# Rounded fp32 products that read and write from the last column to the first

## The chip, the cores and the metric

The kernel runs on one core of a Trainium2 chip. The metric is the device time of one execution in microseconds; lower is better. Beside the time there is a profile of one execution: every instruction of the engines TensorE (PE; its weight loads are listed apart as PEld), VectorE (DVE), ScalarE (ACT), GpSimd (POOL) and SyncE (SP), with the transfers. TensorE reads a stationary and a moving operand from the on-chip memory and adds its results into PSUM, a memory of eight banks of 512 fp32 columns on 128 partitions.

## The reference

One layer of a decoder block over 512 tokens of width 1024, in float32:

```
h = x + 1/2 * SwiGLU_1(RMSNorm(x))                 # D_FF = 2816
z = RMSNorm(h) @ W_in                              # q, three pairs of k/v, gates, S5 input u
o = concat(sparse_attention(z), S5(u)) @ W_out     # 8 heads of 64 in 2 groups; compressed,
h = h + o                                          #   selected and window branches, gated
h = h + 1/2 * SwiGLU_2(RMSNorm(h))
h = h + sigmoid(RMSNorm(h) @ W_gate) * (p @ W_ple)
out = RMSNorm(h)

def swiglu(x, w1, w3, w2):
    return (jax.nn.silu(x @ w1) * (x @ w3)) @ w2
```

Nearly all the arithmetic is in dense products of 128-row weight tiles with activations of 512 tokens.

## The kernel before

Activations lie transposed: features on the 128 partitions, the 512 tokens along the columns. So a product takes a 128x128 weight tile as stationary operand and 512 (or 256) token columns as moving operand, and writes as many columns of a PSUM bank.

To keep the accuracy of fp32, each fp32 operand `x` is split into two rounded fp32 (`float32r`, FR) parts, `hi = round(x)` and `lo = round(x - hi)`; `mm3` then makes three products into one PSUM group: hi with hi, hi with lo, lo with hi. Weights come in units of 128x1024 fp32 (`load_unit`, on ScalarE's DMA queue), are rounded by ScalarE (`hi`, line 164) and subtracted by VectorE (`lo`, line 166). `xh` and `xl` are the two halves of a normed activation, `hq` those of a SwiGLU's hidden tile, `oh` and `ol` those of the mixer's output, `sh` and `sl` those of the sums of blocks of the activation.

The stages in order of time are: the first SwiGLU (about 0 to 365 us, beside it the constants of the S5 mixer on POOL and VectorE), the projections by `W_in` with the S5 scan (365 to 480), the compressed keys and the scores (480 to 555), attention's values (`values`, 555 to 605) with the product by `W_out`, the second SwiGLU (656 to 980), the gate and the last norm. Both SwiGLUs make some of their "up" tiles by a scheme of seven block products in place of eight (`up_fast`): its products have 256 columns, and their results lie in halves of the banks A, B and D. The "down" products have 512 columns and write bank C. The banks are four tags, A to D, with two buffers each (`bank`); a bank is used again when its reader (ScalarE or VectorE) is done.

In `values`, a block of keys takes two products into a bank of tag C (`KA` with `QA`, `KB` with `QB`; a bf16 mask product is added on the diagonal), ScalarE takes the exponential, and two products with `VL` (`eh`, `el`) add to a bank of tag D.

Every product that is not a transpose is issued by the helper `mm`, so they all stand at line 133 in the profile and are told apart by the names of their tiles. The order of work on each engine is set when the program is built, by a scheduler with a cost model of its own, and `pinned` keeps chosen instructions in program order. The same step sets which semaphores an instruction waits for.

Some products are not of the kind that the change names: the bf16 warm-up products (`wz`) and masks, the plain fp32 products of the GLU (`yt` with `raw`) and of the compression (`raw` with `cs` and `turn`), the S5 products, products with 280 columns (values and gates), and transposes (lines 727, 1016, 1162, 1343). Line 1016 transposes the S5 output into PSUM columns that stand eight words apart:

```
p = bank(TP, (128, 64, 8))
for t in range(8):
    PE.transpose(p[:, :, t], yc[:, t], ident[:64, :64])
```

Of the kernel before, what the change touches and what calls it, by code (L numbers as in the profile page):

```python
# [11 lines left out]
FR = mybir.dt.float32r  # L12
# [64 lines left out]
def block_kernel(ctx: ExitStack, tc: tile.TileContext, a: dict, out: bass.AP):  # L77
# [14 lines left out]
    def bank(tag, shape=(128, 512), dt=F32):  # L92
        return psum.tile(list(shape), dt, tag=tag, name="ps_" + tag)
# [36 lines left out]
    pinned = tc.keep_in_program_order  # L130

    def mm(o, lhsT, rhs, start, stop, **kw):
        return PE.matmul(o, lhsT, rhs, start=start, stop=stop, **kw)  # L133


# [5 lines left out]
    for i in range(COLD):  # L141
        pinned(mm(cold, wz[:, :128], wz, True, True))

    def unit(raw_only=False, keep=None, q=nc.scalar, after=None, at=None):
        i = unit_i[0] if at is None else at
        if at is None:
            unit_i[0] += 1
        w = UNIT_W[i]
        if i not in raws:
            load_unit(i, q)  # L150
        raw = raws.pop(i)
        if raw_only:
            return raw
        return split(raw, (slice(0, w),), keep, after)
# [18 lines left out]
    def mm3(o, wh, wl, xh, xl, first, last, kept=free):  # L173
        kept(mm(o, wh, xh, first, False))
        kept(mm(o, wh, xl, False, False))
        kept(mm(o, wl, xh, False, last))
# [1273 lines left out]
    for m in range(KT):  # L1450
        if m % 4 == 0:
            wu = unit()
        o = bank("B")
# [18 lines left out]
    with tc.tile_pool(name="gate", bufs=2, reuse_waits="tile") as gp:  # L1472
# [15 lines left out]
        def products(i, wu, cs, kept=free, beside={}):  # L1488

            o = bank("AB"[i % 2])[:, :cs.stop - cs.start]  # L1490
            for k in range(KT):
                sl = slice(k * 128, (k + 1) * 128)
                for j, (w_, x_) in enumerate(((0, ng.xh), (0, ng.xl), (1, ng.xh))):
                    kept(mm(o, wu[w_][:, sl], x_[:, k, cs], k + j == 0, k == KT - 1 and j == 2))
                if k in beside:
                    beside[k]()
            return o
# [34 lines left out]
        for m in range(KT - 3):  # L1532
            o = products(m, unit(), slice(0, SEQ))
# [246 lines left out]
```

## Time and profile before

| what | value |
|---|---|
| median of three runs | 1042.88 us (1041.19 to 1043.49) |
| span of the profiled execution, first to last instruction | 1040.7 us; its own time outside the profiler is not listed |
| granted TensorE clock, mean | 0.997 |
| TensorE products | 1028.1 us busy, 6048 records |
| TensorE weight loads | 874.7 us, 6049 records |
| VectorE, ScalarE, POOL | 822.9, 506.2 and 161.3 us |
| products of 512 columns into bank C from `hq` | 1056 records, mean 389 to 390 ns each as modelled |
| products of 256 columns | mean 280 to 289 ns each as modelled |

The modelled length of a product is longer than its distance to the next, since products overlap in the array. A group that the timeline merges (x8) has the length from the first start to the last end. A record of a plain fp32 product is one of two in which the chip makes it.

### The profile page before, as it was taken

How to read it: one execution, taken by the hardware profiler on the slowest of the kernel's cores; microseconds unless marked ns; L12 is line 12 of the kernel's file. 1: busy time of each engine (PE TensorE's matmuls, PEld its weight loads, DVE VectorE, ACT ScalarE, POOL GpSimd, SP SyncE). 2: the span in 40 equal slices, each digit the busy share in tenths (PEclk: the TensorE clock that was granted, in tenths of full speed). 3: DMA queues.
4: the chain of work that ended last, by engine and by line, in shares of the span. 5: the costliest groups of instructions: out<-in, count | busy, mean ns of one | idle time of the engine just before them, and what ended most of it. 6: DMA issues, size and time to landing. Idle time of an engine off the chain costs nothing.

```text
span 1040.7 us, 15688 instructions
## 1 busy us (share of the span) xinstructions
PE 1028.1 (99%) x6048; PEld 874.7 (84%) x6049; DVE 822.9 (79%) x1382; ACT 506.2 (49%) x872; POOL 161.3 (15%) x181
## 2 busy tenths in 40 slices
PE   9999999999999999999999999999999999999997
PEld 6888888889889888776586688998999899899886
DVE  6798468988889766986698877996598588687676
ACT  6322232535336542667678855663365245255452
POOL 0003948207870200100000000000000000000001
PEclk9999999999999999999999999999999999999998
DMA  8424325646354639566510023333333333333412
GB/s 267 143 85 134 100 86 168 232 122 129 120 133 151 228 117 226 181 198 181 162 41 21 21 70 127 127 103 121 93 94 118 101 102 102 101 103 104 145 56 82
DMA packets 50618, 129.98 MB, mean 125 GB/s; under 512 B 10608, under 2 KB 17424, under 8 KB 50544
## 3 DMA queue, kind: packets, MB, share of 16 engines
q10 hardware_dynamic: 26352, 90.77, 28.2%
q0 software_dynamic: 6592, 18.48, 7.0%
q1 hardware_dynamic: 17600, 19.73, 6.1%
q8 instruction: 47, 0.77, 0.3%
q14 instruction: 27, 0.22, 0.1%
HBM read 112.81 MB, written 15.73 MB: 124 GB/s over the span
## 4 chain that ended last, share of the span: by engine, by line
PE 89%; DVE 3%; POOL 3%; DMA 2%; issue 2%; ACT 1%; SPq 0%; DVEq 0%; ACTq 0%; POOLq 0%
PE ps_A L133 27%; PE ps_C L133 25%; PE ps_B L133 20%; PE ps_D L133 16%; POOL ft L721 1%; POOL bt L720 1%; DMA raw<-in_wpack 1%; DMA cst<-kcd 0%; DVE lo L166 0%; DMA kcd<-ra 0%; POOL ft L719 0%; DVE s L342 0%; POOL seen L559 0%; DMA h<-in_xT 0%; PE ps_D L727 0%
## 5 line engine op out<-in xcount | busy, mean ns | idle before, releaser
L164 ACT CAST hi<-raw 128x1024 fp32r<-128x1024 f32 (+2 forms) x143 | 144.4, 1010 | 250.3 <-PE ps_C L133 92.6
L133 PE MATMUL ps_C<-hq,hi 128*128 128x512 f32 x704 | 217.6, 390 | 0.2
L166 DVE TENSOR_TENSOR lo<-raw,hi 128x1024 fp32r<-128x1024 f32 (+2 forms) x143 | 174.1, 1218 | 44.5 <-ACT hi L164 43.6
L133 PEld LDWEIGHTS ps_C<-hq,hi 128*128 128x128 f32 x704 | 130.8, 188 | 28.1 <-DVE h L526 1.3
L133 PE MATMUL ps_C<-hq,lo 128*128 128x512 f32 x352 | 136.9, 389 | 0.0
L133 PE MATMUL ps_A<-xh,hi 128*128 128x512 f32 (+1 forms) x352 | 124.5, 354 | 0.5 <-ACT hi L164 0.5
L133 PE MATMUL ps_A<-xl,hi 128*128 128x512 f32 (+1 forms) x352 | 124.1, 352 | 0.4 <-DVE xl L192 0.3
L133 PE MATMUL ps_A<-xh,lo 128*128 128x512 f32 (+1 forms) x352 | 122.5, 351 | 0.2 <-DVE lo L166 0.2
L164 ACT CAST hi<-s 128x1024 fp32r<-128x1024 f32 x56 | 59.0, 1053 | 107.1 <-PE ps_D L133 63.6
L166 DVE TENSOR_TENSOR lo<-s,hi 128x1024 fp32r<-128x1024 f32 x56 | 70.6, 1261 | 20.4 <-ACT hi L164 20.3
L133 PEld LDWEIGHTS ps_C<-hq,lo 128*128 128x128 f32 x352 | 66.1, 188 | 13.8
L133 PEld LDWEIGHTS ps_A<-xh,hi 128*128 128x128 f32 x352 | 66.5, 189 | 10.4 <-ACT hi L164 0.7
L133 PEld LDWEIGHTS ps_A<-xl,hi 128*128 128x128 f32 x352 | 66.5, 189 | 10.1 <-DVE xl L192 1.2
L133 PEld LDWEIGHTS ps_A<-xh,lo 128*128 128x128 f32 x352 | 66.5, 189 | 9.2 <-DVE lo L166 0.4
L526 DVE SCALAR_TENSOR_TENSOR h<-ps_C,h 128x512 f32<-128x512 f32 x64 | 43.9, 686 | 36.8 <-PE ps_C L133 36.6
L133 PE MATMUL ps_B<-sh,lo 128*128 128x256 f32 x224 | 63.1, 282 | 0.3 <-DVE lo L166 0.3
L133 PE MATMUL ps_D<-sl,hi 128*128 128x256 f32 x224 | 63.1, 282 | 0.0
L133 PE MATMUL ps_B<-sh,hi 128*128 128x256 f32 x224 | 63.0, 281 | 0.0
L133 PE MATMUL ps_B<-sl,hi 128*128 128x256 f32 x224 | 62.9, 281 | 0.0
L133 PE MATMUL ps_D<-sh,hi 128*128 128x256 f32 x224 | 62.8, 280 | 0.0
L133 PE MATMUL ps_B<-xh,hi 128*128 128x512 f32 (+1 forms) x168 | 62.8, 374 | 0.0
L133 PE MATMUL ps_D<-sh,lo 128*128 128x256 f32 x224 | 62.7, 280 | 0.0
(435 smaller groups left out, 2470.9 us busy)
## 6 DMA issues: line engine op xcount, KB each, us to landing
raw<-in_wpack ACTq DMA_DIRECT2D x168, 512.0 KB, 3.6
si<-s5i POOLq DMA_DIRECT2D x8, 512.0 KB, 5.2
so<-s5o POOLq DMA_DIRECT2D x8, 512.0 KB, 5.5
h<-in_xT SPq DMA_DIRECT2D x8, 256.0 KB, 4.1
s5i<-fs POOLq DMA_DIRECT2D x1, 2048.0 KB, 11.3
xraw<-in_xT SPq DMA_DIRECT2D x8, 256.0 KB, 3.4
s5o<-gt POOLq DMA_DIRECT2D x1, 2048.0 KB, 13.4
s5i<-tcs POOLq DMA_DIRECT2D x2, 1024.0 KB, 10.4
```

The source lines that it names most:

```text
L133: return PE.matmul(o, lhsT, rhs, start=start, stop=stop, **kw)
L164: p, q = S.copy(hi[:, c], raw[:, c]), None
L166: q = V.tensor_tensor(lo[:, c], raw[:, c], hi[:, c].bitcast(F32), OP.subtract)
L526: V.scalar_tensor_tensor(h[:, m, :], o[m], 0.5, h[:, m, :], OP.mult, OP.add)
L720: G.tensor_tensor(bt, b2[:, 1], bc(psn[:, e]), OP.mult)
L721: G.tensor_tensor(ft[:, :, s_, :], ft[:, :, s_, :], bt, OP.add)
```

## The change

`mm` reverses the column order of both sides of a product where the moving operand is rounded fp32, has two dimensions and 256 or 512 columns. Column n of the moving operand still lands in column n of the result; only the order in which the columns go through the array is turned. The stationary operand is left as it is.

```
     def mm(o, lhsT, rhs, start, stop, **kw):
+        if len(rhs.shape) == 2 and rhs.shape[1] in (256, 512) and rhs.dtype == FR:
+            o, rhs = o[:, ::-1], rhs[:, ::-1]
         return PE.matmul(o, lhsT, rhs, start=start, stop=stop, **kw)
```

Two lines more make line 133 into line 135 in the changed kernel. In the built program the access patterns of 2664 products of 512 columns and of 2496 of 256 columns begin at the last column and have a step of -1. The order of instructions is the same on every engine, and so are the waits of all engines but TensorE. There, waits on TensorE's own semaphore (PE_49) come and go. In the two pieces that follow, each row is a product with its result and operands, and in brackets the semaphores that it waits for.

On TensorE in `values`, at a head group's end and the next one's start, before:

```order
L133 MATMUL ps_D<-eh,VL 128x512 [waits Activation_49]
L133 MATMUL ps_C<-QA,KA 128x512
L133 MATMUL ps_C<-QB,KB 128x512
L133 MATMUL ps_D<-el,VL 128x512 [waits DVE_49]
L133 MATMUL ps_D<-eh,VLc 128x512 [waits PE_49,Activation_49]
```

The same rows of the changed kernel:

```order
L135 MATMUL ps_D<-eh,VL 128x512 [waits Activation_49]
L135 MATMUL ps_C<-QA,KA 128x512 [waits PE_49]
L135 MATMUL ps_C<-QB,KB 128x512
L135 MATMUL ps_D<-el,VL 128x512 [waits DVE_49]
L135 MATMUL ps_D<-eh,VLc 128x512 [waits Activation_49]
```

The first product into a bank of tag C now waits for TensorE's own earlier product there, and the first into the bank of tag D no longer does.

On TensorE in `up_fast`, where a half of bank D begins a new tile, before:

```order
L133 MATMUL ps_A<-xh,hi 128x256
L133 MATMUL ps_A<-xl,hi 128x256
L133 MATMUL ps_A<-xh,lo 128x256
L133 MATMUL ps_D<-sh_1758,hi 128x256
L133 MATMUL ps_D<-sl_1759,hi 128x256
```

The same rows of the changed kernel:

```order
L135 MATMUL ps_A<-xh,hi 128x256
L135 MATMUL ps_A<-xl,hi 128x256
L135 MATMUL ps_A<-xh,lo 128x256
L135 MATMUL ps_D<-sh_1758,hi 128x256 [waits PE_49]
L135 MATMUL ps_D<-sl_1759,hi 128x256
```

Here too the tile's first product waits for the product that last wrote the bank. In all, 63 products get such a wait and 18 lose one.

## The prediction

> **What bounds the kernel now.** I read the page first: its busy shares, its row of granted clock and the chain that ended last.
>
> ```profile
> PE 1028.1 (99%) x6048; PEld 874.7 (84%) x6049; DVE 822.9 (79%) x1382; ACT 506.2 (49%) x872; POOL 161.3 (15%) x181
> ...
> PEclk9999999999999999999999999999999999999998
> ...
> PE 89%; DVE 3%; POOL 3%; DMA 2%; issue 2%; ACT 1%; SPq 0%; DVEq 0%; ACTq 0%; POOLq 0%
> ```
>
> The reader is to see that TensorE is busy for 1028.1 of 1040.7 us at the full granted clock and makes 89% of the chain, so 12.6 us are all its idle time. Whatever a product takes more or less goes into the end time almost one to one: the next engine, VectorE, has 822.9 us of work, 218 us less than the span.
>
> What one product costs is the distance from its start to the next start, not its modelled length (0.28 or 0.39 us). The chain in order of time gives it, since it merges runs of products into one bank:
>
> ```profile
> 226.70 5.44 PE ps_B L133 x24
> 232.14 1.43 PE ps_A L133 x12
> ```
>
> The first row is 24 products of 512 columns: 5.44 / 24 = 0.227 us each. The second is 12 of 256 columns: 0.119 us each. Two reference rates stand beside them, the bf16 warm-up products near the end and the plain fp32 products of the GLU and of the compression:
>
> ```profile
> 1028.86 1.89 PE L133 MATMUL ps_C<-wz 128*128 128x512 bf16 x8
> ...
> L133 PE MATMUL ps_C<-wz x14: 376/378/379, 1028.9 to 1032.0; 128*128 128x512 bf16 x14
> ...
> L133 PE MATMUL ps_A<-yt,raw 128*128 128x512 f32 x32 | 14.8, 601 | 0.0
> ...
> 495.99 3.65 PE L133 MATMUL ps_A<-yt,raw 128*128 128x512 f32 x8
> ...
> 480.55 0.38 PE L133 MATMUL ps_A<-raw,cs 128*64 128x256 f32 x1
> ...
> 480.76 0.38 PE L133 MATMUL ps_A<-raw,cs 128*64 128x256 f32 x1
> ```
>
> Columns of the timeline rows are start, length of the merged group, engine and operation. Eight bf16 products with one 0.378 us tail: (1.89 - 0.38) / 7 = 0.216 us. So 512 columns stream in 0.216 us, and a rounded fp32 product has 0.011 us beyond that; at 256 columns it is the same (0.119 - 0.108). A record of plain fp32 moves at half that rate: (3.65 - 0.60) / 7 = 0.436 us for 512 columns, 480.76 - 480.55 = 0.21 us for 256.
>
> **The change, part by part.** No instruction is added, removed or moved in any engine's work, and no operand has other bytes. Three things differ.
>
> *The steps.* In the built program 2664 products of 512 columns and 2496 of 256 have a step of -1 instead of +1 in moving operand and result; the stationary operand, which PEld loads, keeps +1. In the profile they take 2664 x 0.227 + 2496 x 0.119 = 605 + 297 = 902 us, 87% of the span. Not reversed are all plain fp32 and bf16 products, the products of 280, 384 and 64 columns, and the scores of the early blocks, whose moving operand has three dimensions. If a step of -1 streams like +1, this part costs 5160 x 0 = 0.
>
> No row of before has a moving operand with a step other than +1 inside its runs. The nearest row for the result is the S5 transpose of line 1016, which writes 64 columns to words that stand 32 bytes apart, beside the transpose of line 727, which writes 128 consecutive ones:
>
> ```profile
> 476.63 0.71 PE L1016 MATMUL ps_D<-ident,ysb 64*128 64x64 f32 x8
> ...
> L1016 PE MATMUL ps_D<-ident,ysb x32: 221/223/273, 428.8 to 477.1; 64*128 64x64 f32 x32
> ...
> 131.09 1.09 PE L727 MATMUL ps_D<-ident,ft 128*128 128x128 f32 x8 [0.33 <-POOL ft L721]
> ```
>
> Scattered: (0.71 - 0.22) / 7 = 0.070 us for 64 columns, 1.09 ns a column with the fixed part in it. Consecutive: (1.09 - 0.27) / 7 = 0.117 us for 128, 0.91 ns a column. Taking 0.011 us off each leaves 0.92 and 0.83 ns: a result written word by word costs about a tenth more here, but at a pace half as fast as the rounded products run (0.216 / 512 = 0.42 ns). So these rows bound the price without deciding it. Lower end: 0. Upper end: every column as a word by itself at the whole 1.09 ns, 0.560 us for 512 and 0.280 for 256, which adds 2664 x 0.333 + 2496 x 0.161 = 1289 us and gives 2332 us. I take 0, the end that the contiguous rows give: columns 511, 510, 509 fall into the same short stretches of memory as 509, 510, 511, each stretch visited once and left for good, and only an address circuit that handles +1 alone would make more accesses of it. That is a judgement on the circuit, not a reading, and both ends stay in the chances.
>
> The Trainium skill speaks against this: "PSUM — Partial Sum Buffer", section "Specifications (TRN2)", gives PSUM lines of 8 bytes and says that any access pattern that isn't contiguous slows matmuls significantly. By it, if a step of -1 counts as not contiguous, two results no longer share an access, and the time would be that of the first rival below; the S5 row agrees only weakly, with its tenth.
>
> *The waits of TensorE on itself.* The order shows that TensorE's waits on its own semaphore change: 63 products get one, 18 lose one (39 before, 84 after), and 9 more of these stand as separate semaphore instructions. No wait of another engine changes. Each new wait is for the product that last wrote the PSUM bank about to be reused. Counted in products on TensorE, 36 of them look 36 to 108 products back (FFN, projections, W_out and the gate), 27 look 4 to 18 back (attention). A satisfied wait of this kind exists in before, on the product at 233.41:
>
> ```profile
> 233.29 0.28 PE L133 MATMUL ps_A<-xh,lo 128*128 128x256 f32 x1
> 233.41 0.28 PE L133 MATMUL ps_D<-sh,hi 128*128 128x256 f32 x1
> 233.53 0.28 PE L133 MATMUL ps_D<-sl,hi 128*128 128x256 f32 x1
> ...
> L1016 PEldq EVENT_SEMAPHORE  x1: 51/51/51, 439.6 to 439.6; - x1
> ...
> 439.39 0.40 PE L133 MATMUL ps_A<-xh,lo 128*128 128x512 f32 x1
> 439.62 0.40 PE L133 MATMUL ps_A<-xh,hi 128*128 128x512 f32 x1
> 439.86 0.39 PE L133 MATMUL ps_A<-xl,hi 128*128 128x512 f32 x1
> ...
> 443.82 0.70 PE L1016 MATMUL ps_D<-ident,ysb 64*128 64x64 f32 x8
> ```
>
> It starts 0.12 us after its neighbour, as the next does: cost 0. The 51 ns semaphore instruction for the transposes at 443.82 was done at 439.6, 18 products ahead, and the products around it start 0.23 to 0.24 us apart: hidden too. What is queued behind a waiting product is all of TensorE's later work, so the question is whether the product waited for has ended. With 36 or more products between, and a queue about 18 ahead, it has. With 4 between (the closest of the 27) it ended 0.39 us after its start, while the waiter's turn comes 4 x 0.23 = 0.92 us after it; 0.53 us are left, and a weight load takes 0.19 of them:
>
> ```profile
> 655.95 0.19 PEld L133 LDWEIGHTS ps_B<-xh,hi 128*128 128x128 f32 x1
> ```
>
> Moreover the bank's reader (ScalarE's exponential or VectorE) had to wait for the same product, and TensorE waits for that reader anyway. Cost taken: 0. Upper end, if this cover were gone and each of the 63 stalled until the product before it had drained, with a semaphore instruction each: 63 x (0.39 - 0.227 + 0.051) = 13.5 us. Lower end: the 18 waits that go were satisfied, so nothing comes back.
>
> *Order of the results in time.* A bank's readers wait for the last product of the group as a whole, whose end is the same whichever column comes last. No reader starts earlier or later: 0.
>
> The sum: 0 + 0 + 0. The profiled execution's span is 1040.7 us; the median of the three runs, 1042.88, stands 2.2 us above it, within which lie what is around the span and the spread of the runs (1041.19 to 1043.49). I forecast 1042.9 us, with an own range of 1040 to 1046. About 0.2% (2.1 us) is what a measurement of this kernel can tell from no change.
>
> **The rivals.**
>
> 1. *Half rate: the kernel becomes far slower.* Place: every reversed product. Mechanism: two columns per access go one way only, in the read of the moving operand or the write of the result, and backwards each column is an access of its own. For it: the S5 row's tenth, and that no row shows a backward stream. Against it: the stretches are the same. Price by the plain fp32 records, which run at such a pace: 0.436 - 0.227 = 0.209 us per 512 columns and 0.215 - 0.119 = 0.096 per 256, 2664 x 0.209 + 2496 x 0.096 = 557 + 240 = 797 us; with TensorE already at 99% nothing hides it: 1840 us, where all engines but TensorE would be idle half the time. It decides from the point at which a product loses more than 2.1 us / 5160 = 0.4 ns.
>
> 2. *A few ns per product.* The start or the turn-around of a backward stream costs once more what the 0.011 us of fixed part costs now: 5160 x 0.011 = 57 us, 1100 us. For it: there is such a fixed part, beyond the bf16 row. Against it: it is as large at 256 columns as at 512, which fits something that happens once per product and knows no direction.
>
> 3. *The fixed part goes.* If it came from the meeting of one product's last columns with the next one's first, a new order could remove it: 1042.9 - 57 = 986 us. Against it: forwards and backwards the next product starts at the far end from where the last one stopped, in both cases.
>
> 4. *The new waits bite in attention.* Up to 13.5 us, 1056 us; worked out above. For it: ScalarE and VectorE end waits there already, so TensorE has little queued. Against it: 0.53 us of margin at the closest.
>
> **How the numbers follow.** The forecast has 0.66, half rate or worse 0.17, a few ns 0.05, the waits 0.08, the fixed part gone 0.04. The range takes the forecast with the waits up to 1056 and a few ns up to 1100, together 0.79, and on the other side down to 1037 for a small part of the third rival: 0.8 in all, with half rate outside. Faster by over 0.2%: 0.04 and half of the forecast's own scatter beyond the bound (0.04 of its 0.66), 0.06. Slower: 0.17 + 0.05 + 0.08 + 0.02 = 0.32. Same: 0.62.
>
> **What would show it.** Right: runs of 24 products at 5.44 us and of 12 at 1.43 in the chain; TensorE's busy time and idle time as now; attention (555 to 605 us) at the same 50 us. Half rate: 24 products in about 10 us, products of 512 columns listed longer than 0.39 us, VectorE's share near 45%. A few ns: the same rows at 5.7 and 1.56. Waits: only the stretch from 545 to 605 us grows, with TensorE named as its own releaser. What would make the forecast wrong is the one thing that no row shows, how fast the memories serve a stream that runs backwards.

## The result, and the profile after

The changed kernel takes 1056.25 us (median of four runs, 1055.68 to 1057.05), the kernel before 1043.18 us beside it (four runs, 1041.19 to 1043.53). The ratio is 1.0131, with a 95% interval of 1.0117 to 1.0146: about 13 us slower. (Ratios here and below are the recorded estimates; the quotient of the two medians can differ from them, as 1.0125 does here, and lies inside the interval.) The profiled execution's span grows from 1040.7 to 1055.3 us.

The page of the changed kernel: busy times, the row of granted clock, the chain that ended last by engine, and the costliest group of products (busy us, mean ns of one, idle before it):

```profile
PE 1042.2 (99%) x6049; PEld 874.8 (83%) x6049; DVE 823.7 (78%) x1382; ACT 506.2 (48%) x872; POOL 159.1 (15%) x181
...
PEclk9999999999999999999999999999999999999999
...
PE 84%; DVE 7%; DMA 4%; issue 3%; ACT 1%; POOL 0%; SPq 0%; DVEq 0%; ACTq 0%; POOLq 0%
...
L135 PE MATMUL ps_C<-hq,hi 128*128 128x512 f32 x704 | 222.3, 398 | 0.5 <-DVE h L528 0.4
```

TensorE's busy time grew by 14.1 us, and its idle time (1055.3 - 1042.2 = 13.1 us) stayed about where it was (12.6). The other engines' busy times moved by at most 2.2 us, and the clock is as before. So the time lies in the products themselves. The chain in order of time says in which:

```profile
232.24 5.60 PE ps_B L135 x24
237.84 1.42 PE ps_A L135 x12
...
246.75 10.86 DMA raw<-in_wpack
```

24 products of 512 columns took 5.44 us and now take 5.60: 0.2333 us from start to start, 6.6 ns more each. 12 products of 256 columns take 1.42 in place of 1.43: nothing. TensorE's share of the chain fell from 89% to 84% because the chain now goes another way for a while, through a weight transfer (the last row) and VectorE; TensorE's idle time shows that next to nothing was lost there. Summed over the whole trace, the distances that begin with a product of 512 columns are 646.0 us before and 660.1 after (+14.1), those with 256 columns 311.4 and 309.8 (-1.6).

2664 x 6.6 ns would be 17.6 us, more than was lost. The rest is in products that were at the slower pace already. Attention, three products in each timeline, before:

```profile
572.67 0.40 PE L133 MATMUL ps_D<-el,VL 128*128 128x512 f32 x1
572.91 0.40 PE L133 MATMUL ps_D<-eh,VL 128*128 128x512 f32 x1
573.14 0.40 PE L133 MATMUL ps_C<-QA,KA 128*128 128x512 f32 x1
```

and after:

```profile
582.81 0.40 PE L135 MATMUL ps_D<-el,VL 128*128 128x512 f32 x1
583.04 0.40 PE L135 MATMUL ps_D<-eh,VL 128*128 128x512 f32 x1
583.28 0.40 PE L135 MATMUL ps_C<-QA,KA 128*128 128x512 f32 x1
```

The distances are 0.23 to 0.24 us in both. In the kernel before, the first eight products after a stall (a distance of over 300 ns) have median distances of 228 to 236 ns before the pace settles at 227, and attention stalls all the time: only 23% of its 512-column distances were at or below 228 ns, against 83% ahead of it and 86% behind. So this stage, from product 3000 (536.1 us before, 546.0 after) to product 3300 (608.1 and 618.4), loses 0.4 us. The stretch ahead of it loses 9.9 and the one behind it about 4.

### The profile page after: what moved, and what is told of

The parts are those of the page before. It is cut to its first block, busy times and chain, and to the rows that moved or that the text cites. A ratio compares the mean times of both kernels' runs of the same rounds, so it can differ in the third digit from the quotient of the medians.

```text
span 1055.3 us, 15698 instructions
## 1 busy us (share of the span) xinstructions
PE 1042.2 (99%) x6049; PEld 874.8 (83%) x6049; DVE 823.7 (78%) x1382; ACT 506.2 (48%) x872; POOL 159.1 (15%) x181
## 4 chain that ended last, share of the span: by engine, by line
PE 84%; DVE 7%; DMA 4%; issue 3%; ACT 1%; POOL 0%; SPq 0%; DVEq 0%; ACTq 0%; POOLq 0%
PE ps_C L135 25%; PE ps_A L135 25%; PE ps_B L135 20%; PE ps_D L135 14%; DMA raw<-in_wpack 1%; DVE lo L168 1%; ACT hi L166 1%; DMA kd<-r 1%; DMA cst<-kcd 1%; DMA kf<-kd 0%; DMA kcd<-ra 0%; DVE aa L351 0%; DVE s L344 0%; DVE vv L990 0%; DMA h<-in_xT 0%
## 5 line engine op out<-in xcount | busy, mean ns | idle before, releaser
L135 PE MATMUL ps_C<-hq,hi 128*128 128x512 f32 x704 | 222.3, 398 | 0.5 <-DVE h L528 0.4
L135 PE MATMUL ps_C<-hq,lo 128*128 128x512 f32 x352 | 139.7, 397 | 0.0
L135 PE MATMUL ps_B<-xl,hi 128*128 128x512 f32 (+1 forms) x168 | 63.1, 376 | 0.0
```

## The experiments

The first question was which products, and which side of them, lose the 6.6 ns; the rivals were the new waits and the write. Later runs ask what is special about the pace of 226.7 ns. The kernel before was timed beside each timed kernel, with medians of 1042.6 to 1043.2 us.

### One width at a time

```
-        if len(rhs.shape) == 2 and rhs.shape[1] in (256, 512) and rhs.dtype == FR:
+        if len(rhs.shape) == 2 and rhs.shape[1] == 512 and rhs.dtype == FR:
```

> Products of 512 columns reversed on both sides, those of 256 left forward. Theory S (the stream: in the trace of the changed kernel 24 products of 512 columns take 5.60 us instead of 5.44, 6.6 ns each, and 12 of 256 take 1.42 instead of 1.43) expects the whole loss: 1056 us, +13, within 1.5. Theory W (TensorE's new waits on itself, 13 us over 63 of them, or over the 27 close ones in attention) expects +9 by the 42 new waits that are left, or +13 by the 27 close ones, and products of 512 columns at 5.44 us for 24 outside attention.

The other kernel has 256 in that place.

> Products of 256 columns reversed on both sides, those of 512 left forward. 46 new waits of TensorE on itself, none of them close. S expects no change: 1043 us, within 1.5. W expects +9.5 by 46 of 63 waits, or none if only the close ones count.

With 512 alone: 1056.15 us, 1.0128 [1.0113, 1.0143], the whole loss. With 256 alone: 1041.99 us, 0.9992 [0.9983, 1.0002], none. The chain of the first and, below it, of the second:

```profile
81.01 5.60 PE ps_B L135 x24
```

```profile
79.41 5.44 PE ps_B L135 x24
```

The 512-column kernel also holds all 27 of the close waits in attention, so this pair does not yet separate them from the step.

### The read and the write

The down products alone (1056 of the 2664), one side each:

```
-   mm3(o[m], us[i][0][:, sl], us[i][1][:, sl], *hid[fl[j]], j == 0, ...
+   mm3(o[m], us[i][0][:, sl], us[i][1][:, sl], *(t[:, ::-1] for t in hid[fl[j]]), j == 0, ...
```

> Only the moving operand of the 1056 down products (512 columns, bank C, from hq) is reversed, so their results come out with the tokens in the opposite order; the results' own steps stay +1. No new wait at all. S with the read as the cause expects 1056 x 6.6 ns = +7.0 us, 1050; S with the write as the cause expects 1043; W expects 1043.

```
-   mm3(o[m], us[i][0][:, sl], us[i][1][:, sl], *hid[fl[j]], j == 0, ...
+   mm3(o[m][:, ::-1], us[i][0][:, sl], us[i][1][:, sl], *hid[fl[j]], j == 0, ...
```

> Only the result of the 1056 down products is written backwards, the moving operand is read forward, so again the tokens come out in the opposite order. 7 new waits, none close. S with the write as the cause expects +7.0 us, 1050; S with the read as the cause expects 1043; if both sides add up, 3.5 us in each of the two runs. W expects +1.4 at most.

In both, the down products' results have their tokens in reverse order; the work is the same. The moving operand alone: 1048.34 us, 1.0053 [1.0038, 1.0068]. The result alone: 1042.69 us, 1.0001 [0.9991, 1.001]. The chain of the first shows the loss in its own products only, the up tile in bank B at the old pace:

```profile
79.83 5.44 PE ps_B L133 x24
...
189.79 29.60 PE ps_C L133 x126
```

29.60 us for 126 down products; the chain of the kernel before has, for the same stretch,

```profile
188.25 28.93 PE ps_C L133 x126
```

That is (29.60 - 28.93) / 126 = 5.3 ns more for each. The page of the kernel that turns the result alone keeps the old mean of 390 ns:

```profile
L133 PE MATMUL ps_C<-hq,hi 128*128 128x512 f32 x704 | 217.5, 390 | 0.7 <-DVE h L526 0.5
```

So the loss is in the read of the moving operand, by the ratio 5.5 us / 1056 = 5.2 ns a product, with no new wait in the kernel. It is less than the 7.0 us expected. A backward write costs nothing.

### The product alone

TensorE by itself, four groups of 24 products for nearly every variant, the layer left out, one execution (the layer is left out of the two later kernels of this kind too):

```
def run(name, n, fm, fo, x=x, w=w, count=4, wide=None):
    for g in range(count):
        o = psum.tile([128, 512], F32, tag="AB"[g % 2], name=name)
        for i in range(24):
            wt = w[:, (i % 8) * 128:(i % 8) * 128 + 128]
            ...
            pinned(PE.matmul(r(o[:, :wide or n]), wt, m(x[:, i % 7, :n]), start=i == 0, stop=i == 23))
```

> The layer is left out: TensorE alone makes groups of 24 products, with no other engine at work, in series that change one thing each, and the output is the last bank. Read is the distance from start to start inside a group. Widths 512, 448, 384, 320, 288, 256, 192, 128, forward and backward on both sides. Theory R1 (a backward read costs a fixed part per product): +6 to 7 ns at 512, 448, 384 and 320, nothing at 256 and below, where the weight load of about 116 ns sets the distance. Theory R2 (a backward read costs something per column): +6.6 at 512, +5.8 at 448, +5.0 at 384, +4.1 at 320. Moving operand alone backward: +6.6 by both; result alone: 0. Blocks of 128 columns in descending order with columns ascending inside: 0 if the direction inside a run counts, +6.6 if the start at the far end counts. Pairs in descending order, ascending inside: R2 expects at least +6.6. Direction changed from product to product: half of 6.6 by both. Theory R3 (what counts is where in a memory line the read begins): forward reads that begin 1, 2 or 3 columns further on cost +6.6 like the backward one, and a read that begins 4 further costs 0. Every second column as moving operand (256 of 512): no theory here has a number; a rule that distant columns slow the read would show it as more than 0.12 us. bf16, and plain fp32 backward: R1 expects +6.6 per record. A result with every second column, bf16 and plain fp32: 0.11 and 0.21 us if such a result is free.

Its timeline merges each variant's 96 products. The distance is the row's length less one product's own (0.39 us at 512 columns, 0.28 at 256), divided by 95:

```profile
183.78 11.68 PE L127 MATMUL fwdf<-x,w 128*128 128x256 f32 x96
195.30 11.53 PE L127 MATMUL revf<-x,w 128*128 128x256 f32 x96
...
228.08 10.85 PE L127 MATMUL fwdh<-x,w 128*128 128x128 f32 x96
...
249.49 22.62 PE L127 MATMUL mov<-x,w 128*128 128x512 f32 x96
271.94 21.94 PE L127 MATMUL res<-x,w 128*128 128x512 f32 x96
293.72 22.24 PE L127 MATMUL alt<-x,w 128*128 128x512 f32 x96
315.80 21.92 PE L127 MATMUL blk<-x,w 128*128 128x512 f32 x96
...
381.72 43.68 PE L127 MATMUL eom<-x,w 128*128 128x512 f32 x96
425.23 22.26 PE L127 MATMUL stm<-x,w 128*128 128x256 f32 x96
447.31 21.96 PE L127 MATMUL offs<-x,w 128*128 128x512 f32 x96
469.11 22.57 PE L127 MATMUL rofs<-x,w 128*128 128x512 f32 x96
491.51 22.90 PE L127 MATMUL offt<-x,w 128*128 128x512 f32 x96
514.25 22.78 PE L127 MATMUL roft<-x,w 128*128 128x512 f32 x96
...
671.60 20.88 PE L127 MATMUL fpa<-h,raw 128*128 128x256 f32 x96
692.32 20.88 PE L127 MATMUL fpb<-h,raw 128*128 128x256 f32 x96
713.04 10.64 PE L127 MATMUL bfa<-xb,wb 128*128 128x256 bf16 x96
723.52 20.88 PE L127 MATMUL bfb<-xb,wb 128*128 128x256 bf16 x96
```

- Moving operand alone backward (`mov`): (22.62 - 0.39) / 95 = 234 ns. Result alone (`res`): 227 ns. Every second product backward (`alt`): 230, the mean of the two; the cost belongs to the backward product and not to the change of direction.
- 448 and 384 columns lose 4 ns each (202.7 to 206.7 and 173.6 to 177.8), 320 nothing (146.7 both), 256 gain 1.6 (119.9 to 118.3). So neither theory of the expectation holds, a fixed price for each product or a price per column. Forward, 256, 320, 384 and 512 columns lie on one line, 13 ns and 0.417 ns a column. At 192 and 128 columns the distance stays near 111 ns (`fwdh`), above that line. What sets it there isn't shown: a weight load lasts 188 to 192 ns in this trace, and loads overlap the products.
- bf16 (216 both ways) and plain fp32 (429 a record) lose nothing.
- Pairs of columns in descending order, ascending inside (`prs`): 233, like single columns. Blocks of 128 columns in descending order on both sides (`blk`): 227. Neither the start at the far end nor its descent costs anything.
- The surprise: a *forward* stream that begins one column into its tile (`offt`) takes 237 ns, against 227 from the tile's start (`offs`); backward it is 236 and 233 (`roft`, `rofs`). Begun two, three and four columns in, forward streams take 233.4, 229.6 and 231.7, so the expected return to 227 at four did not come.

The last point upset the theory that descending reads are slow as such: a forward one can be slower still.

### Blocks, and a third of the products

Blocks of 128 columns in descending order in the kernel, with the same 84 waits of TensorE on itself as in the changed kernel:

```
-            o, rhs = o[:, ::-1], rhs[:, ::-1]
+            o, rhs = (t.rearrange("p (b n) -> p b n", n=128)[:, ::-1] for t in (o, rhs))
```

> The same 5160 products take their columns in blocks of 128 from the last block to the first, ascending inside a block, on both sides. TensorE has the same 84 waits on itself as in the changed kernel. Theory D (the read costs more where the columns descend inside a run; a jump back between long runs is free, as in the series alone on TensorE, 0.227 us) expects 1043 us, within 1.5. A theory by which the start at the far end costs expects 1056. W, the waits, expects 1056.

1043.13 us, 0.9998 [0.9988, 1.0007], and its chain is back at

```profile
78.96 5.44 PE ps_B L135 x24
```

This clears the waits: all of them are there, and nothing is lost. Then one of `mm3`'s three products (640 of 512 columns) fully reversed:

```
-        kept(mm(o, wh, xl, False, False))
+        if len(xl.shape) == 2 and xl.shape[1] == 512:
+            kept(mm(o[:, ::-1], wh, xl[:, ::-1], False, False))
+        else:
+            kept(mm(o, wh, xl, False, False))
```

> Of the three products of a split pair made by the common helper only the second (weight hi with activation lo), where it has 512 columns, is reversed on both sides: 640 products among forward ones. D with a price per product expects 640 x 4.9 ns (13.1 us over 2664 in the changed kernel) = +3.1 us, up to 640 x 6.6 = +4.2: 1046 to 1047. If a change of direction between neighbours cost something by itself, it would be more than that; if one forward neighbour were enough to keep the faster pace, 1043.

1047.26 us, 1.0038 [1.0023, 1.0053]: by the ratio +4.0 us, 6.3 ns for each of the 640. Its chain has 8 reversed products of 24, (5.49 - 5.44) / 8 = 6 ns:

```profile
79.96 5.49 PE ps_B L133 x24
```

### Where the operands lie

If a forward stream can be slow too, place may matter. This kernel moves the weights, or the moving operand, by some columns in memory, and descends in runs of 4 to 64 columns:

```
k = d + (i % one) * 128
pinned(PE.matmul(fo(o[:rows, :n]), fw(w2[:, k:k + rows]), fm(x[:, i % 7, :n]), start=i == 0, stop=i == 23))
```

> The layer is left out: TensorE alone, groups of 24 products of 512 columns, forward and with the moving operand backward. Theory P (the read and the next weight load, both 4-byte streams out of the same memory, get in each other's way, and the place in a line at which each begins sets by how much) expects the distance of forward products to move between 0.227 and 0.237 when the weights begin 1, 2, 4, 8, 16 or 32 columns further on, and expects the difference between the directions to shrink with weight tiles of 64 or 32 columns, whose load is shorter. Theory L (the read alone: a backward stream asks for the memory in another order, whatever else reads) expects 0.227 forward and 0.233 backward at every place of the weights and every size of the weight tile. Activations that begin 8, 16, 32 or 64 columns further on: by L forward 0.227 where that keeps to a line's start. Runs of 4, 8, 16, 32, 64 ascending columns in descending order: the shortest run that still gives 0.227 is the length that the read wants in order; D has no number for it beyond that 2 is too short and 128 long enough. 256 columns: 0.116 to 0.120 in all.

From its timeline: weights 8 columns on, forward and backward (`wfe`, `wre`); runs of 32 and of 64 columns in descending order (`blu`, `blv`); the moving operand 32 columns on (`xfl`, `xrl`) and 64 (`xfm`, `xrm`).

```profile
193.41 22.55 PE L131 MATMUL wfe<-x,w 128*128 128x512 f32 x96
215.80 22.56 PE L131 MATMUL wre<-x,w 128*128 128x512 f32 x96
...
484.36 22.47 PE L131 MATMUL blu<-x,w 128*128 128x512 f32 x96
506.66 21.93 PE L131 MATMUL blv<-x,w 128*128 128x512 f32 x96
...
661.77 22.47 PE L131 MATMUL xfl<-x,w 128*128 128x512 f32 x96
684.07 22.88 PE L131 MATMUL xrl<-x,w 128*128 128x512 f32 x96
706.79 21.95 PE L131 MATMUL xfm<-x,w 128*128 128x512 f32 x96
728.57 22.57 PE L131 MATMUL xrm<-x,w 128*128 128x512 f32 x96
```

Weights moved by 8 columns alone bring the forward stream to (22.55 - 0.39) / 95 = 233.3 ns, exactly the backward value; weights moved by 1, 2, 4, 16 or 32 columns give 230.7 to 233.4. Moving operand 64 columns on: 226.9 again, 32 on: 232.4. Descending runs of 64 columns: 226.7, of 32: 232.4, the value of a forward stream that lies 32 columns off; of 16, 8 and 4: 233.4. 64 columns are 256 bytes. That gives the *phase theory*: 226.7 ns is the pace of one arrangement, in which moving operand and weights begin at the same place modulo 256 bytes and both ascend. Out of step the pace is about 233 (229 to 237), and a descending stream doesn't keep step, while descending runs of 64 columns keep the places modulo 256 bytes as they were.

Two things limit the theory. Where a product by itself took 226.7 ns, both operands began at byte 128 modulo 256, in all three of these kernels; no run moves both by the same amount. So a rule for each operand apart (begin at byte 128) fits as well as a rule for the two together, and which it is stays untested. And place is not all: with weight tiles of 64 and 32 columns, in place, forward streams take 230.1 and 231.6 ns and backward ones 233.3. The directions come closer, as the expectation's theory P had it, but because the forward stream loses its fast pace.

In the kernel before, 2456 of the products of 512 columns have weights from the ring and both operands at byte 128 modulo 256. Another 16, with `pl`, have 96 and 128, and take 234 ns (median; their neighbours with `ph`, which are in step, take 228 with `hi` and 232 with `lo`). The other 192, in attention, have both at 128 as well, and no weights from the ring.

### The weights moved in the kernel

The theory says that the kernel can lose its time without any reversal. One number moves the weights' ring by 32 bytes; instructions, their order and their waits are the same on every engine:

```
-PADS = 320, 0, 224, 24832, 60
+PADS = 272, 0, 224, 24832, 60
```

> The kernel before, every product forward, with the weights' ring and all that lies beside it moved 32 bytes (8 columns) in memory: 2456 of the 2664 products of 512 columns then read a moving operand and weights that begin 32 bytes apart modulo 256, where both began at the same place. Nothing else differs, no instruction and no wait. Phase theory (226.7 ns needs moving operand and weights in step modulo 256 bytes; out of step it is about 233 ns whichever way one reads): the products by themselves gave 233.3 ns at this offset, so the whole loss appears without any reversal, 1042.6 + 2456 x 5.1 ns = about 1055 us, and chains of 24 take 5.60 us in place of 5.44. Direction theory (descending reads are slower, whatever the place): no change, 1042.6 us within 2, chains 5.44.

The same edit in the changed kernel:

> The same move of the weights by 32 bytes, in the changed kernel (256 and 512 columns from the last to the first). Phase theory: already out of step by its direction, it loses nothing more: about 1056 us, 233 ns a product, like the changed kernel and like the move alone. A theory in which offset and direction cost apart and add up: about 1056 + 12.5 = 1068.5 us, about 240 ns a product. Direction theory: 1056 us too, but then the move alone stays at 1042.6.

And 256 bytes, 64 in place of 320, with every product forward (three waits on VectorE and ScalarE then stand one instruction from where they stood):

> The kernel before, every product forward, with the weights' ring and all that lies beside it moved by 256 bytes (64 columns), the full period, in place of 32 bytes. Phase theory: moving operand and weights are in step again, so nothing is lost: 1042.6 us within 2, chains of 24 in 5.44 us. Rival (the 32-byte move cost by being a move: other neighbours in memory, other arrivals of the weights' transfers): it loses too, 1048 to 1055 us.

| kernel | us | ratio to before | 512 columns, sum us | 256 columns, sum us |
|---|---|---|---|---|
| before (profiled execution) | 1043.2 | 1 | 646.0 | 311.4 |
| changed | 1056.25 | 1.0131 [1.0117, 1.0146] | 660.1 | 309.8 |
| weights moved 32 bytes, forward | 1053.2 | 1.0095 [1.0077, 1.0113] | 659.7 | 307.5 |
| weights moved 32 bytes, backward | 1056.2 | 1.0124 [1.0108, 1.0141] | 660.5 | 309.2 |
| weights moved 256 bytes, forward | 1043.43 | 1.0004 [0.9995, 1.0014] | 647.4 | 311.4 |

The sums are distances from start to start in each trace. The three chains, in the table's order (32 bytes forward with one tile of 256 columns, 32 bytes backward, 256 bytes):

```profile
80.43 5.60 PE ps_B L133 x24
...
237.16 1.41 PE ps_A L133 x12
```

```profile
81.38 5.60 PE ps_B L135 x24
```

```profile
79.80 5.44 PE ps_B L133 x24
```

A forward kernel with its weights 32 bytes further on loses 13.7 us in its 512-column products, as much as the reversal (14.1), and the two together lose no more than either (14.5). A move by 256 bytes loses nothing, so the move itself, with its other neighbours and transfers, isn't the cause. The time of the first came out at 1053.2 and not at the 1055 expected, since its 256-column products became 3.9 us faster. 3.0 us of it are in the 1344 products with `sh` and `sl`, whose two operands stood 32 bytes apart and now stand 64 apart; about 1 us is in 816 products that were in step and now aren't. So at 256 columns the arrangement that is best at 512 isn't best, and why is open. Nor does the rule say why the 16 `pl` products, now 64 bytes apart, take 228 ns here.

### The map of places

> TensorE alone on rounded fp32, the layer left out; groups of 24 products, the moving operand 0 to 60 columns (steps of 4) into its tile, weights in place or 32 columns on, forward and backward. Phase theory: at 512 columns forward 226.7 ns at offset 0 alone and 230 to 237 elsewhere, with no offset near half of 64 columns as fast as 0; backward 230 to 240 at every offset; with 256 columns the pace of the weights (111 to 120 ns) rules and backward is within 2 ns of forward at most offsets. Direction theory: forward 227 at every offset, backward 233 at every one.

Its timeline, 48 products a row, the moving operand 0 (`sa`, `ra`), 4 (`sb`, `rb`), 16 (`se`, `re`) and 32 columns (`si`, `ri`) into its tile, s forward and r backward:

```profile
286.87 11.09 PE L131 MATMUL sa<-x,w 128*128 128x512 f32 x48
297.80 11.37 PE L131 MATMUL ra<-x,w 128*128 128x512 f32 x48
309.00 11.28 PE L131 MATMUL sb<-x,w 128*128 128x512 f32 x48
320.12 11.37 PE L131 MATMUL rb<-x,w 128*128 128x512 f32 x48
...
376.13 11.15 PE L131 MATMUL se<-x,w 128*128 128x512 f32 x48
387.12 11.36 PE L131 MATMUL re<-x,w 128*128 128x512 f32 x48
...
465.31 11.36 PE L131 MATMUL si<-x,w 128*128 128x512 f32 x48
476.51 11.36 PE L131 MATMUL ri<-x,w 128*128 128x512 f32 x48
```

Forward, the sixteen offsets give 227.6 ns at 0 and 228.9 to 235.9 elsewhere; backward all sixteen give 233.3 to 233.5. So a backward stream has no good place among them, and a forward one has a best place that the kernel before had. How far two runs agree is seen at 32 columns: backward 233.3 here (`ri`) and 236.7 in the kernel ahead (`xrl`), so 3 ns between two single rows can be scatter. At offset 0 the rows of the three kernels agree far better, 226.7 to 227.6 forward (the first row of a kernel apart, which has its start-up in it) and 233.3 to 233.9 backward. With 256 columns the offsets scatter, forward from 114 to 120 ns (from 116 to 127 at offsets of 1 to 7 columns that aren't multiples of 4), backward from 118 to 120, with no rule that I could read.

## Why the prediction was right or wrong

The time, 1056.25 us, lies inside the range of 1037 to 1100, but the forecast itself, no change at 1042.9, was wrong by 13 us, and "slower" had 0.32. That the range holds it is luck: it reached so far up for the waits and for a fixed price on each product, and neither is what cost the time.

- **What bounds the kernel: right.** What the products took more went into the end time one to one (14.1 us of TensorE's busy time, 14.6 of span).
- **The steps, taken as 0: this is the term that failed.** It is about +14 us for 512 columns and -1.6 for 256. The prediction argued that backward columns fall into the same short stretches of memory, each left for good. That looked at one operand by itself. The pace goes by the places of two operands: moving the weights by 32 bytes costs as much as turning the moving stream (233.3 against 226.7 ns, by place alone). The rows chosen as bounds, the S5 transposes, were about the write, which turned out free; for the read there was no row, and 0 was a judgement.
- **The page's rule.** The Trainium skill, "PSUM — Partial Sum Buffer", section "Specifications (TRN2)", says that an access pattern that isn't contiguous slows matmuls significantly. For a step of 2 the runs agree in bf16: results of 256 columns go from (10.64 - 0.28) / 95 = 109 ns (`bfa`) to (20.88 - 0.38) / 95 = 216 (`bfb`); in plain fp32 they don't (216 both, `fpa` and `fpb`). For a step of -1 they show no such price: 227 ns (`res`), and 1.0001 [0.9991, 1.001] in the kernel. If the page's rule holds, a descending run counts as contiguous by it.
- **The waits, taken as 0: right.** Attention lost 0.4 us, and the blocks kernel carries the same waits at 0.9998. The rival on the waits named 1056 us, the right number by the wrong way.
- **The order of the results, 0: right** (the same 1.0001).
- **The rivals.** Half rate: nowhere near; a step of -1 isn't served like a step of 2, which does halve the pace of the read ((43.68 - 0.6) / 95 = 453 ns for 512 columns, `eom`). A few ns per product, with 0.05, was the nearest, at 57 us against 13: the 11 ns taken for each of 5160 products were 6.6 for the 512-column ones that ran undisturbed, and none for the 256-column ones. Its mechanism is not what was found: the start at the far end is free (`blk`), the turn-around is free (`alt`), and a forward stream pays as much for its place. The argument against it, that the fixed part is as large at 256 columns as at 512, was right as a reading (11 ns above bf16 at both, 226.7 - 216 and 119.9 - 109), but the conclusion does not follow: the backward price depends on the width, 6.6 ns at 512, 4 at 384 and 0 at 320. The third rival found nothing: no variant of the rounded fp32 product had a mean below 226.7 ns at 512 columns.
- **The signs.** Asked for: 5.44 and 1.43, or for a few ns 5.7 and 1.56. Found: 5.60 and 1.42. Idle time and attention stayed as forecast.

What stays open is why. The period of 256 bytes, and that moving either operand costs about the same, suggest that the read of the moving operand and the load of the next weights meet somewhere. No run shows where, nor why 320 columns and fewer pay nothing, nor why the products after a stall start at up to 236 ns.

## What to carry to other kernels

When a change turns or shifts an operand, ask what else reads the memory at that moment, and compare the new start with the other operand's (here modulo 256 bytes), not only with its own old pattern; before pricing an edit that moves no work, look in the old profile for products of the same kind that already run slower (here those of attention and with `pl`, at about 234 ns). For a TensorE-bound kernel in rounded fp32 with 512 columns, begin moving tiles and weight tiles at the same place modulo 256 bytes (byte 128 here; no other common place was tried) and let both ascend: that was worth 1% here, and costs only padding. Before taking a step at 0 because no row speaks against it, look for which of its two sides, read and write, has no row at all.

## What the runs showed of the hardware

- Rounded fp32, 512 columns, weight tiles of 128 columns: 226.7 ns where both operands begin at byte 128 modulo 256 and ascend, 229 to 237 at the other places tried; backward 233.3 to 233.5 at all sixteen offsets of the last map (236.7 at 32 columns in the second of these kernels, up to 240 at single odd offsets in the first). From 320 columns down, from the tile's start, the two directions are within 1.6 ns of each other.
- At 192 and 128 columns, with 128x128 weights, a rounded fp32 product comes about 111 ns after the one before it in both directions.
- A result written backward is free; a result with a step of 2 halves the pace in bf16 (109 to 216 ns at 256 columns) and costs nothing in plain fp32 (`fpa` and `fpb`, (20.88 - 0.38) / 95 = 216 ns a record both).
- A moving operand in rounded fp32 with a step of 2 halves the pace: 453 against 227 ns at 512 columns, 230 against 120 at 256 (`stm`, (22.26 - 0.41) / 95).
- No version of the layer that was tried was faster than the kernel before by more than the noise. The 3.9 us that the 256-column products gained with the weights 32 bytes on suggest one that keeps the 512-column operands in step and moves only those of 256; it was not run.
